# Linear attention over 256 tokens: scores about the middle of each 128 tokens and one block between the halves, in place of chunk states and transposed keys

## The chip, the cores and the metric

The kernel runs on one core of a Trainium2 chip. A core has an engine for matrix products (TensorE, PE in the profile, whose loads of stationary weights are listed apart as PEld), VectorE (DVE), ScalarE (ACT), GpSimd (POOL) and SyncE (SP), which here issues nearly all transfers. Each engine works through its own queue in order, and waits on semaphores for the others. The metric is the device time of one execution in microseconds (us); smaller is better.

## The reference, cut to what matters

One decoder layer over 256 tokens of width 1024: a norm with modulation, a wide projection, two mixing branches, a mixture of 64 experts, and a last norm. The change lies in the first branch, gated linear attention with 4 heads (keys of 128, values of 256):

```python
log_a = jax.nn.log_sigmoid(g_dn @ gate_w2 + gate_b) / GATE_TAU      # per token and key channel
b = jnp.cumsum(gc, axis=3)                  # gc: log_a in chunks of 64 tokens
q_t = qc * jnp.exp(b)
k_t = kc * jnp.exp(-b)
k_s = kc * jnp.exp(b_last - b)
attn = jnp.where(causal, jnp.einsum('nbhid,nbhjd->nbhij', q_t, k_t), 0.0)
o_intra = jnp.einsum('nbhij,nbhjv->nbhiv', attn, vc)
# over the chunks, one after the other, from S = 0:
o_i = jnp.einsum('bhid,bhdv->bhiv', q_i, state)
state = d_i[..., None] * state + jnp.einsum('bhid,bhiv->bhdv', k_i, v_i)
# output: o_intra + o_inter
```

So token t sees token s at or before t through the product of all decays between them. The code scales q by 1/sqrt(128) as well. What follows (norm per head, gate, output products, experts) is the same in both kernels.

## The kernel before, in words

All weights are read from HBM once, in an order fixed by hand. SP's queue holds every load in that order, and a load is issued when its slot in SBUF comes free. The projections run over a list of 88 items, each a 128x1024 block of weights. Each item from 16 on is 24 matmuls of 256 columns (`mm_blk`, L356). Five items ahead of its use (`LA`), a block is split into a high and a low part: `split_h` is a cast on ACT (L340), `split_l` a subtraction on DVE (L347) that also frees the block's ring slot. DVE further does one reduction over a block of the modulation weights in many items (`mod_blk`, L257).

Work between items is hung on item numbers. In the loop over items, `first(b, f)` runs ahead of the splits that stand in item b, `pre(b, f)` after the cast and ahead of the DVE half of the splits, and `at(b, f)` after both and ahead of item b's own matmuls:

```python
run((b, "first"))
for nxt in nxts: split_h(nxt)
if pend: evac(b, *pend)
run((b, "pre"))
for nxt in nxts: split_l(nxt)
run(b)
mm_blk(b, ps[:, i % 2], rhs)
```

The attention is hung on items 16 to 39. `gate0` to `gate4` make `bb`, the running sum of the gate in chunks of 64. `gate5` to `gate8` make three arrays of exponentials on ACT: `eb` (L453) for q, `enb` (L463) for the keys of the scores, and `ekb` (L464, after a subtraction on DVE, L456) for the keys of the states; `decay` holds a chunk's last value. `k_evac` (L720, L721) and `q_evac` (L715) multiply the projections in PSUM by them. Then TensorE transposes the state keys (`gla_kst`, L481), makes the scores of each 128 tokens (`gla_attn`, L494), which DVE copies under a mask (`gla_attn2`, L498), makes three state products (`gla_state`, L506), which ACT and DVE chain up (L513, L515), and the outputs per head: values by scores (L525) and states by queries, one 64-token chunk at a time (L529).

Four PSUM tiles M0 to M3 are handed out in turn by `mt`: the transposes take two, the scores two, the state products of the first two chunks all four, so those wait until the scores have been copied.

After the items follow the router and the experts, in groups of four: a product of 12 loads of 2 MB (`l1_unit`, `l2_unit`, L1044), whose slots are refilled as soon as a product is done with them.

Of the kernel before, what the change touches and what calls it, by code (L numbers as in the profile page):

```python
# [7 lines left out]
F32 = mybir.dt.float32  # L8
# [4 lines left out]
AF = mybir.ActivationFunctionType  # L13
OP = mybir.AluOpType
# [5 lines left out]
TT = 2  # L20
H = 4
# [96 lines left out]
def trunk_kernel(ctx: ExitStack, tc: tile.TileContext, xT: bass.AP, c: bass.AP, modw: bass.AP,  # L118
# [29 lines left out]
    def fl(t):  # L148
        return t.rearrange("p a b -> p (a b)")
# [78 lines left out]
    ident = sm.tile([128, 128], F32, name="ident")  # L228
    V.tensor_scalar(ident, jp, 0.0, None, op0=OP.is_equal)
    cmask = sm.tile([128, 128], I32, name="cmask")  # L230
    V.tensor_scalar(cmask, jp, 0.0, None, op0=OP.is_ge)
    V.memset(cmask[0:64, 64:128], 0)
    tri = sm.tile([128, 128], BF, name="tri")
    V.tensor_scalar(tri, jp, 0.0, None, op0=OP.is_gt)
    trif = sm.tile([128, 128], BF, name="trif")
# [58 lines left out]
    for i in range(2):  # L294
        ps = mt()
# [107 lines left out]
    L = {}  # L403


    t9 = big.tile([128, 4, 1024], F32, name="t9", tag="T9")
    gb = big.tile([128, 4, H, TOK], F32, name="gb", tag="T10")
    la, bb, eb, enb = (t9[:, i].rearrange("p (h t) -> p h t", h=H) for i in range(4))
    L["sr"], L["osq"] = (t9[:, 2 * i:2 * i + 2].rearrange("p a (k t) -> p (a k) t", t=TOK) for i in range(2))
    L["v"] = t8[:, 0].rearrange("p (t d) -> p t d", t=2)  # L410
    L["o"] = gb[:, 2:4].rearrange("p a h t -> p (a h) t")
    ekb, qt, kt_, ks = (gb[:, i] for i in range(4))
    decay = sm.tile([128, H, 4], F32, name="decay")
    b4 = bb.rearrange("p h (c t) -> p (h c) t", t=64)

    def gate0():
        ps = zt(512)
# [32 lines left out]
        V.tensor_tensor_scan(fl(bb), smask, fl(la), 0.0, op0=OP.mult, op1=OP.add)  # L450

    def gate5():
        S.activation(eb, bb, AF.Exp, scale=-1.0 / 16)  # L453

    def gate6():
        V.tensor_sub(ekb.rearrange("p h (c t) -> p (h c) t", t=64),  # L456
                     b4[:, :, 63:64].to_broadcast([128, 16, 64]), b4)

    def gate7():
        V.tensor_copy(decay, eb.rearrange("p h (c t) -> p h c t", t=64)[:, :, :, 63])  # L460

    def gate8():
        S.activation(enb, bb, AF.Exp, scale=1.0 / 16)  # L463
        S.activation(ekb, ekb, AF.Exp, scale=-1.0 / 16)  # L464

    def gla_setup():
        g2 = big.tile([128, 4, 1024], F32, name="gc", tag="T11")
        L["kst"] = g2[:, 0].rearrange("p (t d) -> p t d", t=2)  # L470
        L["at"] = g2[:, 1].rearrange("p (t h i) -> p t h i", t=2, h=H)
        for ch, i in ((1, 2), (2, 3), (3, 0)):
            L["S", ch] = g2[:, i].rearrange("p (h d) -> p h d", h=H)
        G.memset(g2[:, 1], 0.0)

    def gla_kst():
        L["pk"] = []
        for tt in range(TT):
            ps = mt(H, 128)
            for h in range(H):  # L480
                T.transpose(ps[:, h], ks[:, h, 128 * tt:128 * tt + 128], ident)  # L481
            L["pk"].append(ps)

    def gla_kst2():
        for tt in range(TT):
            S.copy(L["kst"][:, tt], fl(L["pk"][tt]))

    def gla_attn():
        L["pa"] = []
        for tt in range(TT):  # L490
# [6 lines left out]
    def gla_attn2(tt):
        V.copy_predicated(L["at"][:, tt], cmask[:, None, :].to_broadcast([128, H, 128]), L["pa"][tt])  # L498

    def gla_state(*chs):  # L500
        for ch in chs:
            L["ps", ch] = [mt(2, 256) for _ in range(2)]
        for h in range(H):
            for ch in chs:
                tt, r = ch // 2, slice(64 * (ch % 2), 64 * (ch % 2) + 64)
                T.matmul(L["ps", ch][h // 2][:, h % 2], L["kst"][r, tt, 128 * h:128 * h + 128],  # L506
                         L["v"][r, tt, 256 * h:256 * h + 256], start=True, stop=True)

    def gla_state2(ch):
        new = L["S", ch + 1]  # L510
        for h in range(H):
            if ch == 0:
                S.copy(new[:, h], L["ps", ch][h // 2][:, h % 2])  # L513
            else:
                V.scalar_tensor_tensor(new[:, h], L["S", ch][:, h], decay[:, h, ch:ch + 1],  # L515
                                       L["ps", ch][h // 2][:, h % 2], op0=OP.mult, op1=OP.add)
# [188 lines left out]
    pk, pq = ([pm.tile([128, 2, TOK], F32, name="m", tag=f"M{2 * j + i}") for i in range(2)] for j in range(2))  # L705
    ps = None
# [5 lines left out]

    def q_evac():
        for j in range(2):
            V.scalar_tensor_tensor(qt[:, 2 * j:2 * j + 2], pq[j], 128.0 ** -0.5, eb[:, 2 * j:2 * j + 2],  # L715
                                   op0=OP.mult, op1=OP.mult)

    def k_evac(j):
        s = slice(2 * j, 2 * j + 2)
        V.tensor_mul(ks[:, s], pk[j], ekb[:, s])  # L720
        V.tensor_mul(kt_[:, s], pk[j], enb[:, s])  # L721

    def b_evac(q, ps):
        if q == 0:
# [142 lines left out]
    o = [0]  # L867
# [82 lines left out]
    pa = ctx.enter_context(tc.tile_pool(name="pa", bufs=2, space=bass.MemoryType.PSUM))  # L950
# [199 lines left out]
    for g in range(NGRP):  # L1150
# [28 lines left out]
        ps = pa.tile([128, D], F32, name="a")  # L1179
# [137 lines left out]
```

## Time and profile before

| | before |
|---|---|
| median of 3 runs | 1206.52 us (1205.83 to 1207.27) |
| profiled execution, its own time | 1206.66 us |
| span of its trace | 1204.8 us |
| PE busy | 902.7 us (75%) |
| DVE busy | 380.0 us (32%) |
| ACT busy | 224.6 us (19%) |
| read from HBM | 475.79 MB, 396 GB/s over the span |
| mean granted TensorE clock | 0.897 of full speed |

The span runs from the first to the last instruction; the execution's own time is 1.86 us longer. "Busy" sums an engine's work over the whole span, so it mixes the projections (to about 297 us) with the experts. In the rows below a time stands in us from the start of the span, and L with a number is a line of the kernel before. One f32 matmul of the code leaves two MATMUL records in the trace, so a group of 8 matmuls reads x16 there.

### The profile page before, as it was taken

How to read it: one execution, taken by the hardware profiler on the slowest of the kernel's cores; microseconds unless marked ns; L12 is line 12 of the kernel's file. 1: busy time of each engine (PE TensorE's matmuls, PEld its weight loads, DVE VectorE, ACT ScalarE, POOL GpSimd, SP SyncE). 2: the span in 40 equal slices, each digit the busy share in tenths (PEclk: the TensorE clock that was granted, in tenths of full speed). 3: DMA queues.
4: the chain of work that ended last, by engine and by line, in shares of the span. 5: the costliest groups of instructions: out<-in, count | busy, mean ns of one | idle time of the engine just before them, and what ended most of it. 6: DMA issues, size and time to landing. Idle time of an engine off the chain costs nothing.

```text
span 1204.8 us, 14633 instructions
## 1 busy us (share of the span) xinstructions
PE 902.7 (75%) x6202; PEld 479.9 (40%) x6202; DVE 380.0 (32%) x718; ACT 224.6 (19%) x375; POOL 3.9 (0%) x15
## 2 busy tenths in 40 slices
PE   9999999999898666666666757576757566757565
PEld 6999999999342212121212212121212111412112
DVE  8968699654431111111111112020202001202103
ACT  6774545433310101010101000000000000100002
POOL 0000000000000000000000000000000000000000
PEclk9999999999999888888888788888888888988888
DMA  9987589978999999999999999999999999999995
GB/s 369 396 333 252 178 301 341 377 272 349 417 428 431 430 431 429 432 431 430 430 430 431 430 431 429 431 430 430 431 429 432 430 432 431 429 430 430 432 427 228
DMA packets 51482, 477.84 MB, mean 397 GB/s; under 512 B 5970, under 2 KB 6098, under 8 KB 27092
## 3 DMA queue, kind: packets, MB, share of 16 engines
q1 hardware_dynamic: 50544, 475.81, 95.4%
q8 instruction: 50, 0.82, 0.2%
q10 hardware_dynamic: 868, 1.05, 0.2%
q14 instruction: 20, 0.16, 0.0%
HBM read 475.79 MB, written 1.05 MB: 396 GB/s over the span
## 4 chain that ended last, share of the span: by engine, by line
DMA 67%; PE 29%; DVE 3%; ACT 0%; issue 0%; DVEq 0%; SPq 0%; ACTq 0%
DMA unit<-in_ew_dram 47%; DMA ring<-in_ew_dram 19%; PE z L356 17%; PE a L1044 3%; PE m L364 2%; PE z L373 2%; PE m L1016 1%; PE m L1071 1%; PE a L1196 0%; PE z L220 0%; PE m L529 0%; PE m L506 0%; PE m L525 0%; PE m L296 0%; DVE xt L257 0%
## 5 line engine op out<-in xcount | busy, mean ns | idle before, releaser
L1044 PE MATMUL a<-unit,xt 128*32 128x512 f32 x1440 | 210.8, 717 | 95.2 <-DMA unit<-in_ew_dram 95.2
L1044 PE MATMUL a<-unit,gt 128*32 128x512 f32 x736 | 119.7, 786 | 70.0 <-DMA unit<-in_ew_dram 69.3
L1044 PEld LDWEIGHTS a<-unit,xt 128*32 128x32 f32 x1440 | 45.0, 122 | 244.0 <-DMA unit<-in_ew_dram 131.5
L356 PE MATMUL z<-hhl,sp 128*128 128x256 f32 x1152 | 140.9, 284 | 0.0
L356 PEld LDWEIGHTS z<-hhl,sp 128*128 128x128 f32 x1152 | 138.9, 192 | 1.6 <-issue 1.5
L1020 ACT ACTIVATE xt<-m,modc,A 128x128 f32<-128x128 f32 x64 | 25.9, 453 | 527.7 <-PE m L1016 526.7
L347 DVE TENSOR_TENSOR sp<-ring,sp 128x1024 fp32r<-128x1024 f32 x88 | 106.9, 1221 | 42.8 <-ACT sp L340 41.8
L1044 PE MATMUL a<-ring,xt 128*32 128x512 f32 x608 | 84.2, 677 | 40.0 <-DMA ring<-in_ew_dram 40.0
L340 ACT CAST sp<-ring 128x1024 fp32r<-128x1024 f32 x88 | 91.4, 1048 | 95.3 <-PE z L356 68.4
L1075 DVE TENSOR_TENSOR wk<-wk,m 128x512 f32<-128x512 f32 (+2 forms) x64 | 41.7, 654 | 196.1 <-PE m L1071 196.1
L1062 DVE TENSOR_TENSOR xt<-a,xt 128x1024 f32<-128x1024 f32 (+3 forms) x19 | 20.0, 1055 | 259.9 <-PE a L1044 253.1
L1044 PEld LDWEIGHTS a<-unit,gt 128*32 128x32 f32 x736 | 24.3, 128 | 154.7 <-DMA unit<-in_ew_dram 99.4
L1016 PEld LDWEIGHTS m<-scr,wk 128*128 128x128 f32 x512 | 60.3, 196 | 21.0 <-issue 20.6
L1016 PE MATMUL m<-scr,wk 128*128 128x128 f32 x512 | 64.0, 283 | 5.6 <-DVE scr L1005 4.9
L1071 PE MATMUL m<-xt,pwt 128*128 128x512 f32 (+2 forms) x136 | 62.7, 603 | 5.3 <-DVE xt L1062 5.3
L1052 DVE TENSOR_TENSOR gt<-gt,a 128x512 f32<-128x512 f32 x16 | 11.0, 688 | 166.3 <-ACT gt L1051 166.3
L257 DVE SCALAR_TENSOR_TENSOR xt<-ring,xt 128x1024 f32<-128x1024 f32 x48 | 58.5, 1219 | 0.3
L1044 PEld LDWEIGHTS a<-ring,xt 128*32 128x32 f32 x608 | 18.6, 117 | 99.2 <-DMA ring<-in_ew_dram 49.8
L1022 DVE TENSOR_SCALAR xt<-m,A,modc 128x128 f32<-128x128 f32 x64 | 23.3, 406 | 105.1 <-PE m L1016 105.1
L1044 PE MATMUL a<-ring,gt 128*32 128x512 f32 x208 | 34.3, 790 | 24.5 <-DMA ring<-in_ew_dram 23.8
L1071 PEld LDWEIGHTS m<-xt,pwt 128*128 128x128 f32 x136 | 25.3, 201 | 49.1 <-issue 36.9
L1051 ACT ACTIVATE gt<-a 128x512 f32<-128x512 f32 x16 | 9.6, 597 | 176.0 <-PE a L1044 176.0
(253 smaller groups left out, 634.9 us busy)
## 6 DMA issues: line engine op xcount, KB each, us to landing
unit<-in_ew_dram SPq DMA_DIRECT2D x136, 2048.0 KB, 38.8
ring<-in_ew_dram SPq DMA_DIRECT2D x48, 2048.0 KB, 38.9
ring<-in_win_dram SPq DMA_DIRECT2D x88, 512.0 KB, 8.0
ring<-in_modw_dram SPq DMA_DIRECT2D x48, 512.0 KB, 6.6
ring<-in_ew_dram SPq DMA_DIRECT2D x12, 512.0 KB, 7.8
unit<-in_el_dram SPq DMA_DIRECT2D x4, 1024.0 KB, 31.5
ring<-in_el_dram SPq DMA_DIRECT2D x4, 512.0 KB, 20.2
unit<-in_el_dram SPq DMA_DIRECT2D x4, 512.0 KB, 11.2
```

Source lines behind the costliest of these rows:

```text
L257: V.scalar_tensor_tensor(scr, st.block("m", i, b), 1.0, cB, op0=OP.mult, op1=OP.mult, accum_out=modc[:, 4 * i + b:4 * i + b + 1])
L340: S.copy(sp(b)[:, 0], st.block("w", n, i))
L347: V.tensor_sub(t[:, 1], st.block("w", n, i), t[:, 0].bitcast(F32))
L356: T.matmul(ps, t[:, ws, k], rhs[rs][:, k], start=(clear and k == 0 and n == 0), stop=(k == KT - 1 and n == 2), skip_group_check=True)
L364: T.matmul(pb[:, h % 2], t[:, ws, h], hl[rs][:, kk], start=(kk == 0 and h % 2 == 0 and n == 0), stop=(kk == KT - 1 and h % 2 == 1 and n == ...
L373: T.matmul(pv[tt][hh], hl[rs][:, kk, 128 * tt:128 * tt + 128], t[:, ws, 512 * hh:512 * hh + 512], start=(kk == 0 and n == 0), stop=(kk == ...
L1016: T.matmul(ps[j], acc[:, tt, f:f + 128], Pm[:, tt], start=(tt == 0), stop=(tt == 1))
L1020: S.activation(xg[:, k], ps[j], AF.Identity, bias=B2[:, k:k + 1], scale=A2[:, k:k + 1])
L1022: V.tensor_scalar(xg[:, k], ps[j], A2[:, k:k + 1], B2[:, k:k + 1], op0=OP.mult, op1=OP.add)
L1044: T.matmul(ps[32 * j:32 * j + 32, 512 * hh:512 * hh + 512], lhsT[:, 32 * j:32 * j + 32], w[:, j, 512 * hh:512 * hh + 512], start=first, st ...
L1071: T.matmul(ps[:, :w], pwt[:, tt], X["y"][:, s], start=True, stop=True)
L1075: V.tensor_add(total[:, tt, s], total[:, tt, s], ps[:, :w])
```

## The change

The chunks of 64 with their running sums stay up to `bb`. From there:

- In each 128 tokens q and k are scaled about the middle (the end of its first 64) instead of the start of their own chunk: `wE` is the distance to the middle in the first half, `bb` itself in the second, and `eq` and `ek` are the exponentials of it with either sign. So one scaled q (`qx`) and one scaled k (`kx`) serve all scores within 128 tokens, also those between its two chunks.
- The block of scores between the first 128 tokens (keys) and the second (queries) comes from `kd` and `qd`: `kx` of the first half times the decay from its middle to its end, and `qx` of the second times the decay of its first chunk (`gla_far`).
- `gla_attn` makes the scores of each 128 tokens in two matmuls per head (keys 0 to 63 by queries 0 to 63, all keys by queries 64 to 127), then the block between the halves in one per head. DVE copies the first kind under the causal mask (`gla_near`, two copies per 128 tokens), ACT copies the block whole (`gla_cross`).
- Each output is then values by scores alone: the values of the first 128 tokens by 256 query columns, those of the second by 128 (`gla_o`).
- The transposes, the copies of transposed keys, the state products, their chaining on ACT and DVE, one array of exponentials, and the second product per key evacuation go.

```diff
-    V.memset(cmask[0:64, 64:128], 0)
...
     def gate5():
-        S.activation(eb, bb, AF.Exp, scale=-1.0 / 16)
+
+        V.tensor_sub(wE, half(bb, 0)[:, :, 63:64].to_broadcast([128, 8, 64]), half(bb, 0))
 
     def gate6():
-        V.tensor_sub(ekb.rearrange("p h (c t) -> p (h c) t", t=64),
-                     b4[:, :, 63:64].to_broadcast([128, 16, 64]), b4)
-
-    def gate7():
-        V.tensor_copy(decay, eb.rearrange("p h (c t) -> p h c t", t=64)[:, :, :, 63])
-
-    def gate8():
-        S.activation(enb, bb, AF.Exp, scale=1.0 / 16)
-        S.activation(ekb, ekb, AF.Exp, scale=-1.0 / 16)
+        for d, sg in ((ek, -1.0), (eq, 1.0)):
+            S.activation(half(d, 0), wE, AF.Exp, scale=sg / 16)
+            S.activation(half(d, 1), half(bb, 1), AF.Exp, scale=-sg / 16)
+        for c in range(2):
+            S.activation(decay[:, c], bb[:, :, 64 * c + 127], AF.Exp, scale=-1.0 / 16)
...
+    def gla_far():
+        for d, x, c, o in ((kd, kx, 0, 0), (qd, qx, 1, 128)):
+            V.tensor_mul(d, x[:, :, o:o + 128], decay[:, c, :, None].to_broadcast([128, H, 128]))
+
+    def gla_attn():
+        L["pa"] = []
+        a, b = slice(0, 128), slice(128, 256)
+        for k, q in ((kx[:, :, a], qx[:, :, a]), (kx[:, :, b], qx[:, :, b]), (kd, qd)):
             ps = mt(H, 128)
             for h in range(H):
-                T.transpose(ps[:, h], ks[:, h, 128 * tt:128 * tt + 128], ident)
...
+                if k is kd:
+                    T.matmul(ps[:, h], k[:, h], q[:, h], start=True, stop=True)
+                    continue
+                T.matmul(ps[0:64, h, 0:64], k[:, h, 0:64], q[:, h, 0:64], start=True, stop=True, skip_group_check=True)
+                T.matmul(ps[:, h, 64:128], k[:, h], q[:, h, 64:128], start=True, stop=True, skip_group_check=True)
             L["pa"].append(ps)
...
+    def gla_near(tt):
+        t, ps = (L["at0"][:, :, 0:128], L["at1"])[tt], L["pa"][tt]
+        for n, c in ((64, 0), (128, 64)):
+            V.copy_predicated(t[:n, :, c:c + 64], cmask[:n, None, c:c + 64].to_broadcast([n, H, 64]), ps[:n, :, c:c + 64])
+
+    def gla_cross():
+        S.copy(L["at0"][:, :, 128:256], L["pa"][2])
...
         for a in range(2):
             f = 256 * h + 128 * a
-            for tt in range(TT):
-                s = slice(128 * tt, 128 * tt + 128)
-                T.matmul(ps[:, a, s], vt[:, tt, f:f + 128], L["at"][:, tt, h],
-                         start=(a == 0 and tt == 0), stop=False, skip_group_check=True)
-            for ch in range(1, 4):
-                s = slice(64 * ch, 64 * ch + 64)
-                T.matmul(ps[:, a, s], L["S", ch][:, h, 128 * a:128 * a + 128], qt[:, h, s],
-                         start=False, stop=(a == 1 and ch == 3), skip_group_check=True)
+            T.matmul(ps[:, a], vt[:, 0, f:f + 128], L["at0"][:, h], start=(a == 0), stop=False, skip_group_check=True)
+            T.matmul(ps[:, a, 128:256], vt[:, 1, f:f + 128], L["at1"][:, h], start=False, stop=(a == 1),
+                     skip_group_check=True)
...
-    at(21, gate6)
-    first(22, gate5)
-    first(23, gate8)
-    at(23, gate7)
+    at(21, gate5)
+    first(22, gate6)
     at(23, lambda: k_evac(0))
     at(24, lambda: k_evac(1))
     at(25, lambda: q_evac())
     at(25, gla_setup)
+    at(26, gla_far)
     at(40, st.free, "T12")
-    at(27, gla_kst)
-    at(28, gla_attn)
-    first(28, gla_kst2)
-    pre(29, gla_attn2, 0)
-    pre(29, gla_attn2, 1)
-    at(29, gla_state, 0, 1)
-    first(30, gla_state2, 0)
-    pre(30, gla_state2, 1)
-    at(31, gla_state, 2)
-    pre(32, gla_state2, 2)
+    at(27, gla_attn)
+    first(28, gla_cross)
+    pre(29, gla_near, 0)
+    pre(29, gla_near, 1)
     at(33, gla_o, 0)
     at(33, gla_o, 1)
...
     def k_evac(j):
         s = slice(2 * j, 2 * j + 2)
-        V.tensor_mul(ks[:, s], pk[j], ekb[:, s])
-        V.tensor_mul(kt_[:, s], pk[j], enb[:, s])
+        V.tensor_mul(kx[:, s], pk[j], ek[:, s])
```

On ACT, in items 21 to 23 (t_181, t_180: the tile of `bb` and the exponentials; t_126, t_125: the projections' results; gb: the tile of the scaled q and k). Before:

```order
L453 ACT_TABLE_LOAD [waits DVE_49]
L453 ACTIVATE t_181<-t_181 128x1024 [waits Activation_49]
L340 CAST sp<-ring 128x1024 [waits DMAHW7_49,PE_49]
L711 COPY t_126<-z 128x512 [waits PE_49]
L463 ACTIVATE t_181<-t_181 128x1024
L464 ACTIVATE gb<-gb 128x1024 [waits DVE_49]
L340 CAST sp<-ring 128x1024 [waits DMAHW1_49,PE_49]
```

and now:

```order
L463 ACT_TABLE_LOAD
L463 ACTIVATE t_180<-gb 128x8x64 [waits DVE_49]
L464 ACTIVATE t_180<-t_180 128x8x64 [waits Activation_49]
L463 ACTIVATE t_180<-gb 128x8x64
L464 ACTIVATE t_180<-t_180 128x8x64
L466 ACTIVATE decay<-t_180 128x4 x2
L339 CAST sp<-ring 128x1024 [waits DMAHW7_49,PE_49]
L683 COPY t_125<-z 128x512 [waits PE_49]
L339 CAST sp<-ring 128x1024 [waits DMAHW1_49,PE_49]
```

All exponentials now stand ahead of the cast of item 27, where one stood there and two behind it; the first waits for DVE's subtraction, and the table load no longer waits for DVE.

On DVE, in items 21 to 26 (L347 and L346: the splits of items 27 on; m: the projections of q and k in PSUM). Before:

```order
L456 TENSOR_TENSOR gb<-t_181 128x1024 [waits DVE_49]
L347 TENSOR_TENSOR sp<-ring,sp 128x1024 [waits DMAHW7_49,PE_49,Activation_49]
L257 SCALAR_TENSOR_TENSOR xt,modc<-ring,xt 128x1024 [waits DMAHW0_49]
L347 TENSOR_TENSOR sp<-ring,sp 128x1024 [waits DMAHW1_49,PE_49,Activation_49]
L460 COPY decay<-t_181 128x16
L720 TENSOR_TENSOR gb<-m,gb 128x512 [waits DVE_49]
L721 TENSOR_TENSOR gb<-m,t_181 128x512
L347 TENSOR_TENSOR sp<-ring,sp 128x1024 [waits DMAHW2_49,PE_49,Activation_49]
L720 TENSOR_TENSOR gb<-m,gb 128x512
L721 TENSOR_TENSOR gb<-m,t_181 128x512
L347 TENSOR_TENSOR sp<-ring,sp 128x1024 [waits DMAHW3_49,PE_49,Activation_49]
L715 SCALAR_TENSOR_TENSOR gb<-m,t_181 128x512 x2
```

and now:

```order
L459 TENSOR_TENSOR gb<-t_180 128x512 [waits DVE_49]
L346 TENSOR_TENSOR sp<-ring,sp 128x1024 [waits DMAHW7_49,PE_49,Activation_49]
L256 SCALAR_TENSOR_TENSOR xt,modc<-ring,xt 128x1024 [waits DMAHW0_49]
L346 TENSOR_TENSOR sp<-ring,sp 128x1024 [waits DMAHW1_49,PE_49,Activation_49]
L692 TENSOR_TENSOR gb<-m,t_180 128x512
L346 TENSOR_TENSOR sp<-ring,sp 128x1024 [waits DMAHW2_49,PE_49,Activation_49]
L692 TENSOR_TENSOR gb<-m,t_180 128x512
L346 TENSOR_TENSOR sp<-ring,sp 128x1024 [waits DMAHW3_49,PE_49,Activation_49]
L687 SCALAR_TENSOR_TENSOR gb<-m,t_180 128x512 x2
L346 TENSOR_TENSOR sp<-ring,sp 128x1024 [waits DMAHW4_49,PE_49,Activation_49]
L479 TENSOR_TENSOR gb<-gb,decay 128x512 [waits DVE_49] x2
```

The subtraction is half as long, each key evacuation is one product instead of two, and the two products of `gla_far` (L479) follow one split behind the queries.

On TensorE, in items 27 to 33, 24 matmuls of L356 (L355 now) to an item (hhl: the normed input, gc: scores, states and transposed keys, t_126 and t_125: values). Before:

```order
L356 MATMUL z<-hhl,sp 128x256 x240
L481 MATMUL m<-ident,gb 128x128 x8
L356 MATMUL z<-hhl,sp 128x256 x24
L494 MATMUL m<-gb 128x128 x8
L356 MATMUL z<-hhl,sp 128x256 x24
L506 MATMUL m<-t_126,gc 128x256 x8
L356 MATMUL z<-hhl,sp 128x256 x48
L506 MATMUL m<-t_126,gc 128x256 x4
L356 MATMUL z<-hhl,sp 128x256 x48
L525 MATMUL m<-gc,t_126 128x128 x2
L529 MATMUL m<-gb,gc 128x64 x3
```

and now (the pair L490, L491 stands there eight times, the pair L507, L508 four times on each side of item 33):

```order
L355 MATMUL z<-hhl,sp 128x256 x240
L490 MATMUL m<-gb 64x64
L491 MATMUL m<-gb 128x64
...
L488 MATMUL m<-gb 128x128 x4
L355 MATMUL z<-hhl,sp 128x256 x144
L507 MATMUL m<-gc,t_125 128x256
L508 MATMUL m<-gc,t_125 128x128
```

All scores now stand ahead of item 27, where the transposes stood, one item earlier than before; nothing stands between items 27 and 32; and a pair of outputs is two matmuls in place of five.

## Rows read from the trace of the kernel before

**Rows 1.** The page's chain of work that ended last, shares by engine.

```profile
DMA 67%; PE 29%; DVE 3%; ACT 0%; issue 0%; DVEq 0%; SPq 0%; ACTq 0%
```

**Rows 2.** That chain in order of time: start, us, what.

```profile
66.30 28.24 PE z L356 x236
...
104.42 0.74 DVE gc L498
105.20 1.99 PE m L506 x14
...
113.12 1.92 PE m L506 x8
...
121.44 0.62 PE m L529 x6
122.05 0.50 PE m L525 x4
...
365.42 29.28 DMA unit<-in_ew_dram
```

**Rows 3.** Windows: us, busy PE, PEld, DVE, ACT, POOL; PEclk, DMA share, GB/s.

```profile
100.00:105.00 5.00, 4.11 (x32) 3.57 (x30) 4.96 (x8) 1.33 (x2) 0.00 (x0) 1.00 0.89 275
...
110.00:120.00 10.00, 10.00 (x77) 9.36 (x76) 6.06 (x9) 4.14 (x5) 0.00 (x0) 1.00 0.65 206
...
365.00:400.00 35.00, 28.56 (x222) 10.69 (x215) 6.60 (x13) 2.35 (x6) 0.00 (x0) 0.97 1.01 430
```

**Rows 4.** Timeline of TensorE, 94 to 104 us: start, us, engine, line.

```profile
94.92 1.04 PE L481 MATMUL m<-ident,gb 128*128 128x128 f32 x8
95.72 3.11 PE L356 MATMUL z<-hhl,sp 128*128 128x256 f32 x24
98.67 1.95 PE L494 MATMUL m<-gb 128*128 128x128 f32 x16
100.37 3.11 PE L356 MATMUL z<-hhl,sp 128*128 128x256 f32 x24
103.41 0.70 PE L506 MATMUL m<-t,gc 64*128 64x256 f32 x2
```

**Rows 5.** Timeline of DVE, 83 to 98 us.

```profile
83.48 1.20 DVE L347 TENSOR_TENSOR sp<-ring,sp 128x1024 fp32r<-128x1024 f32 x1
84.60 1.22 DVE L456 TENSOR_TENSOR gb<-t 128x1024 f32<-128x1024 f32 x1
...
88.11 1.22 DVE L257 SCALAR_TENSOR_TENSOR xt<-ring,xt 128x1024 f32<-128x1024 f32 x1
...
96.18 1.28 DVE L715 SCALAR_TENSOR_TENSOR gb<-m,t 128x512 f32<-128x512 f32 x2
```

**Rows 6.** Timeline of ACT, 83 to 87 us.

```profile
83.65 1.28 ACT L453 ACT_TABLE_LOAD   x1 [3.43 <-DVE t L450]
84.94 1.06 ACT L453 ACTIVATE t<-t 128x1024 f32<-128x1024 f32 x1
85.91 1.03 ACT L340 CAST sp<-ring 128x1024 fp32r<-128x1024 f32 x1
```

**Rows 7.** Groups of ACT by line and form: busy us, mean ns.

```profile
L567 ACT CAST ohl<-gb 128x512 fp32r<-128x512 f32 x4 | 2.5, 615 | 0.0
...
L669 ACT ACTIVATE dum<-epsc 128x1 f32<-128x1 f32 x1 | 0.2, 203 | 0.0
```

**Rows 8.** Windows of 1 us in the first group of experts; columns as in rows 3.

```profile
322.00:323.00 1.00, 0.56 (x8) 0.00 (x0) 0.00 (x0) 0.37 (x1) 0.00 (x0) 1.00 1.11 475
323.00:324.00 1.00, 0.00 (x0) 0.00 (x0) 0.74 (x2) 0.23 (x1) 0.00 (x0) 1.00 0.99 426
...
326.00:327.00 1.00, 1.00 (x8) 0.22 (x4) 0.93 (x10) 0.00 (x0) 0.00 (x0) 0.57 0.99 426
327.00:328.00 1.00, 1.00 (x9) 0.22 (x5) 0.93 (x5) 0.00 (x0) 0.00 (x0) 0.50 0.92 393
...
329.00:330.00 1.00, 1.00 (x12) 0.20 (x8) 0.97 (x2) 0.00 (x0) 0.00 (x0) 0.73 1.07 459
```

More of the change, by code (lines that the diff above doesn't have):

```diff
@@ L407, in trunk_kernel @@
     gb = big.tile([128, 4, H, TOK], F32, name="gb", tag="T10")
-    la, bb, eb, enb = (t9[:, i].rearrange("p (h t) -> p h t", h=H) for i in range(4))
+    la, bb, eq, ek = (t9[:, i].rearrange("p (h t) -> p h t", h=H) for i in range(4))
     L["sr"], L["osq"] = (t9[:, 2 * i:2 * i + 2].rearrange("p a (k t) -> p (a k) t", t=TOK) for i in range(2))
@@ L411, in trunk_kernel, with half @@
     L["o"] = gb[:, 2:4].rearrange("p a h t -> p (a h) t")
-    ekb, qt, kt_, ks = (gb[:, i] for i in range(4))
-    decay = sm.tile([128, H, 4], F32, name="decay")
-    b4 = bb.rearrange("p h (c t) -> p (h c) t", t=64)
+    wE, qx, kx = gb[:, 0, 0:2].rearrange("p h t -> p (h t)"), gb[:, 1], gb[:, 3]
+    wE = wE.rearrange("p (a t) -> p a t", t=64)
+    kd, qd = (gb[:, 2].rearrange("p h t -> p (h t)")[:, 512 * i:512 * i + 512].rearrange("p (h t) -> p h t", h=H)
+              for i in range(2))
+    decay = sm.tile([128, 2, H], F32, name="decay")
+    def half(t, c):
+        return t.rearrange("p h (a c t) -> p (h a) c t", c=2, t=64)[:, :, c]
     def gate0():
@@ L468, in gla_setup @@
+        for c in range(2):
+            S.activation(decay[:, c], bb[:, :, 64 * c + 127], AF.Exp, scale=-1.0 / 16)
     def gla_setup():
         g2 = big.tile([128, 4, 1024], F32, name="gc", tag="T11")
[L470 to L477, printed above, removed]
-        for tt in range(TT):
+        L["at0"] = g2[:, 0].rearrange("p (h i) -> p h i", h=H)
@@ new lines, in gla_setup @@
+        L["at1"] = g2[:, 1, 0:512].rearrange("p (h i) -> p h i", h=H)
+        G.memset(L["at0"][:, :, 0:128], 0.0)
+        G.memset(L["at1"], 0.0)
+    def gla_far():
[5 more added lines that the diff above has]
+        for k, q in ((kx[:, :, a], qx[:, :, a]), (kx[:, :, b], qx[:, :, b]), (kd, qd)):
@@ L479, in gla_kst @@
             ps = mt(H, 128)
             for h in range(H):
-                T.transpose(ps[:, h], ks[:, h, 128 * tt:128 * tt + 128], ident)
[L482 to L490, printed above, removed]
-            s = slice(128 * tt, 128 * tt + 128)
-            ps = mt(H, 128)
-            for h in range(H):
-                T.matmul(ps[:, h], kt_[:, h, s], qt[:, h, s], start=True, stop=True)
-            L["pa"].append(ps)
@@ L497, in gla_attn2 @@
[L497 to L516, printed above, removed]
+                if k is kd:
+                    T.matmul(ps[:, h], k[:, h], q[:, h], start=True, stop=True)
+                    continue
@@ L522, in gla_o @@
             f = 256 * h + 128 * a
-            for tt in range(TT):
-                s = slice(128 * tt, 128 * tt + 128)
-                T.matmul(ps[:, a, s], vt[:, tt, f:f + 128], L["at"][:, tt, h],
-                         start=(a == 0 and tt == 0), stop=False, skip_group_check=True)
-            for ch in range(1, 4):
-                s = slice(64 * ch, 64 * ch + 64)
-                T.matmul(ps[:, a, s], L["S", ch][:, h, 128 * a:128 * a + 128], qt[:, h, s],
-                         start=False, stop=(a == 1 and ch == 3), skip_group_check=True)
+            T.matmul(ps[:, a], vt[:, 0, f:f + 128], L["at0"][:, h], start=(a == 0), stop=False, skip_group_check=True)
+            T.matmul(ps[:, a, 128:256], vt[:, 1, f:f + 128], L["at1"][:, h], start=False, stop=(a == 1),
+                     skip_group_check=True)
         L["po", h] = ps
@@ L714, in q_evac @@
         for j in range(2):
-            V.scalar_tensor_tensor(qt[:, 2 * j:2 * j + 2], pq[j], 128.0 ** -0.5, eb[:, 2 * j:2 * j + 2],
+            V.scalar_tensor_tensor(qx[:, 2 * j:2 * j + 2], pq[j], 128.0 ** -0.5, eq[:, 2 * j:2 * j + 2],
                                    op0=OP.mult, op1=OP.mult)
```

## The prediction

> **What bounds the kernel now.** I read the chain of waits first, then windows of the stretch that the change touches, then the timelines of three engines there. By the chain 67% of the span is DMA and 29% TensorE [rows 1]. In order of time the two do not alternate: up to 362 us the chain runs almost wholly through TensorE, and from 365.42 us on the transfers of expert weights end it [rows 2]. The windows say the same: at 365 to 400 us the DMA engines move 430 GB/s and are full, while at 110 to 120 us they move 206 GB/s, although TensorE is busy for all of that stretch [rows 3]. There the loads wait for slots, and slots come free at TensorE's pace.
>
> So a microsecond taken from TensorE before the loads fill the DMA engines makes every later load start that much earlier, and the end should move by the same amount. A shorter DVE or ACT instruction gives nothing by itself; it counts where TensorE waits for it. That happens once in the attention: the state products begin at 103.41 us, stop, and go on at 105.20 us, because DVE's masked copy of the scores (L498) starts at 104.42 us only, and the products need the PSUM tiles that it frees [rows 2, 4].
>
> **What is removed.** Transposes: 94.92 to 95.72, 0.80 us. Old scores: 98.67 to 100.37, 1.70 us, or 0.106 us for each of 16 records of 128 columns [rows 4]. State products: from 103.41 to 105.20 + 1.99 = 107.19, which is 3.78 us with the stop in it, and 1.92 us for the third chunk [rows 2, 4]. Outputs: a pair is 0.50 + 0.62 us, and there are 8 (4 heads, two halves of the values): 8.96 us [rows 2]. Together 0.80 + 1.70 + 3.78 + 1.92 + 8.96 = 17.16 us of TensorE's line.
>
> The chaining of states on ACT and DVE, the second key products and the copies of transposed keys go too. Outside the stop they lie beside TensorE, so I cost them at nothing. They matter only through the times at which the new scores can start.
>
> **What is added: the outputs.** A pair is now one matmul of 256 columns and one of 128, two records each. For 128 columns I take 0.106 to 0.125 us a record (the 1.70/16 above; 0.50/4 of L525). For 256 columns the lower bound is twice 0.106, the upper 0.24, which is 1.92/8 of the third state product [rows 2]. A pair is 0.64 to 0.73 us, eight are 5.1 to 5.8; I take 5.4, between, since these weights have 128 rows and those of L506 64.
>
> **What is added: the scores.** They stand where the transposes stood, at 94.92 us, and need `kx` and `qx`. When are these ready? I follow the order of rows on ACT and DVE with the durations of before.
>
> DVE's subtraction starts as before at 84.60 us; half as long, it ends near 85.3 (one of two operations of 512 columns is 1.28/2 us at L715) [rows 5]. The exponentials wait for it. The table load does not wait any more: before, it ran at 83.65 only when DVE was through, and took 1.28 us [rows 6]; now it has room ahead of 85.3. An ACT instruction of 512 columns takes 0.615 us [rows 7], and successive ones overlap by about 0.1 us (84.94 + 1.06 against 85.91 [rows 6]). Four of them, the second waiting for the first, end at about 87.6, and two of four columns, at most 0.2 us each by the small one in [rows 7], bring ACT to 87.9. There the cast of item 27 starts, which began at 85.91 before: 2.0 us later. Its 1.03 us over [rows 6], DVE goes on at 88.95.
>
> DVE then does a split (1.12 us from start to start, 83.48 to 84.60), a reduction (1.2), a split, half of the keys (0.6), a split, the other half, a split, and the queries in two parts of 0.6 [rows 5]. That is 88.95 + 1.12 + 1.2 + 1.12 + 0.6 + 1.12 + 0.6 + 1.12 = 95.8, the first half of q at 96.5, the second at 97.1. Before, the queries started at 96.18 [rows 5]: what DVE saves on the keys and what it waits longer for the cast nearly cancel. The first two heads need the first half alone. So TensorE, there at 94.92, stands until about 96.6: a new wait of 1.7 us. Queued behind it are the splits' consumers, item 27 and all that follows; the casts on ACT that wait for TensorE to leave a slot start later too, but five items of lead cover that (an item is 24 x 28.24/236 = 2.87 us [rows 2]).
>
> The 8 pairs of near scores are 32 records of 64 columns. L529 has that form: 0.62/6 = 0.103 us a record [rows 2], no less than 128 columns take, so its weight loads set the pace. Half of the new ones load 64 columns of weights only. If that halves their time, 32 cost 2.5 us, if not, 3.3; I take 2.9, to 99.5 us.
>
> [...]
>
> Meanwhile DVE does a split and the two products of `gla_far`: 97.1 + 1.12 + 0.6 + 0.7 = 99.5. So the block between the halves just meets its operands, and its 8 records of 0.106 us bring the scores to 100.4 us. A faster near part would gain nothing, since DVE then ends last. Scores: 100.4 − 94.92 = 5.5 us.
>
> The copies of the scores no longer hold anyone: the outputs stand six items on, some 17 us later. Two memsets on POOL replace one, in item 25, four items ahead of the copies. SP's loads keep their order.
>
> **Sum.** 17.16 − 5.4 − 5.5 = 6.2 us less. The profiled execution took 1206.66 us by its own time, 0.14 us above the median of the runs. Forecast: 1206.66 − 6.2 = 1200.5 us.
>
> **The rivals.**
>
> *The clock falls in the new wait.* [...] Against it: the stop at 104 us, hardly shorter than the new one, left the clock at 1.00 [rows 3]. [...]
>
> *A longer wait for q.* If ACT's exponentials over columns in pieces of 64 cost more, or the table load still follows the subtraction (1.28 us), the wait is 3 us: 4.9 us saved, 1201.8; with dear outputs and near scores (0.4 us each), 1202.6.
>
> *No wait at all.* Without the later cast, the first half of q would be ready at 96.18 + 0.6 − 1.2 (two key products) − 0.6 (half a subtraction) = 95.0 us [rows 5], `gla_far` at 95.6 + 1.12 + 1.3 = 98.0 and the scores at 98.9. Then 7.7 us are saved, 8.0 with cheap outputs: 1198.7. [rows 6] speak against it: the cast stands behind all exponentials.
>
> *The gain is not handed on.* If the loads bound the end by their own rate from earlier than I think, the change ends at 1206.5, give or take. For it: 67% of the chain is DMA [rows 1]. Against it: 206 GB/s at 110 to 120 us against 430 at the end [rows 3].
>
> [...]
>
> **How the numbers follow.** Forecast case 0.58; the clock 0.15; a longer wait 0.10; no wait 0.07; not handed on 0.07; slower 0.03. Faster by over 0.2% are the first four, 0.90; the same 0.07; slower 0.03. The range takes in the clock, the longer wait with dear matmuls and a part of their sum, and on the other side most of the case without a wait: 1198.8 to 1203.6 us.
>
> **What would show it.** Right: TensorE idle once for 1 to 2.5 us just ahead of the near scores, released by the q product on DVE; none ahead of the outputs; a pair of outputs near 0.67 us; item 34 starting at 100.4 + 7 x 2.87 + 5.4 = 125.9 us; from there the same work at the same distances, the switch of the chain to DMA at 365.4 − 6.2 = 359 us. Wrong: a granted clock under 1.00 between 95 and 130 us, a second stop ahead of the block between the halves, or later stretches that give the 6 us back as lower DMA rates. What would break the forecast most is a wait ahead of the near scores much longer than DVE's queue explains.

## The result, and the profile after

| | before | changed |
|---|---|---|
| median of 6 runs | 1207.17 us | 1213.14 us (1209.57 to 1213.60) |
| ratio to before, 95% interval | | 1.0051 [1.0041, 1.0061] |
| span of the profiled execution | 1204.8 us | 1211.7 us |
| mean granted TensorE clock | 0.897 | 0.886 |
| read from HBM | 475.79 MB, 396 GB/s | 475.79 MB, 394 GB/s |

The change makes the kernel 6 us slower where 6 us faster was forecast. Lines in the rows below are those of the kernel that they come from. In the changed one L355 is the matmuls of the items, L490 and L491 the near scores (64 and 128 columns of weights), L488 the far block, L507 and L508 the outputs, L1015 the experts.

The chain of waits of the changed kernel in order of time (start, us, what) answers to [rows 2]:

```profile
66.68 25.80 PE z L355 x215
...
96.04 0.61 DVE gb L687
96.69 0.33 PE m L490 x2
...
104.02 1.81 PE m L488 x8
105.84 18.45 PE z L355 x144
...
132.40 5.75 PE z L355 x48
...
363.84 31.91 DMA unit<-in_ew_dram
```

In the same view of the kernel before, item 34 starts here:

```profile
132.74 5.80 PE z L356 x48
```

The reader sees the new wait (L490 follows DVE's L687), scores that take until 105.84 us, and item 34 at 132.40 us. Before, item 34 starts at 132.74 us, though its items began 0.38 us earlier (66.30 [rows 2] against 66.68). So the whole attention, 17 us of removed work and all, gave some 0.7 us in these two executions. And the 7 us by which the span is longer arise later still: the chain leaves TensorE at 363.84 us, earlier than before, but that load lands at 395.75 us against 365.42 + 29.28 = 394.70 [rows 2], and from there on the loads alone make the chain, up to 1180.5 us (in the kernel before up to 1172.8).

The windows (columns as in [rows 3]) show both places:

```profile
95.00:100.00 5.00, 3.77 (x21) 2.88 (x21) 5.00 (x7) 1.61 (x3) 0.00 (x0) 0.82 0.97 333
100.00:105.00 5.00, 5.00 (x22) 4.18 (x23) 3.00 (x5) 0.00 (x0) 0.00 (x0) 0.50 0.81 243
105.00:110.00 5.00, 5.00 (x31) 5.00 (x31) 0.00 (x0) 0.78 (x2) 0.00 (x0) 0.66 0.48 185
...
365.00:400.00 35.00, 27.29 (x205) 9.24 (x194) 6.13 (x12) 1.99 (x4) 0.00 (x0) 0.95 1.01 426
```

From about 98 to 108 us TensorE is granted 0.50 of full speed: (1 − 0.82) x 5 / 0.5 + 5 + (1 − 0.66) x 5 / 0.5 = 10.2 us at the low level, so 5.1 us of work at the full clock is lost. And at 365 to 400 us the DMA engines, as full as before, move 426 GB/s instead of 430 [rows 3].

On TensorE's timeline the near scores begin at one pace and go on at another:

```profile
96.69 0.33 PE L490 MATMUL m<-gb 128*64 128x64 f32 x2 [1.23 <-DVE gb L687]
96.95 0.43 PE L491 MATMUL m<-gb 128*128 128x64 f32 x2
97.32 0.33 PE L490 MATMUL m<-gb 128*64 128x64 f32 x2
...
98.82 0.48 PE L490 MATMUL m<-gb 128*64 128x64 f32 x2
...
99.85 0.48 PE L490 MATMUL m<-gb 128*64 128x64 f32 x2
...
124.13 0.60 PE L507 MATMUL m<-gc,t 128*128 128x256 f32 x2
124.56 0.38 PE L508 MATMUL m<-gc,t 128*128 128x128 f32 x2
124.78 0.60 PE L507 MATMUL m<-gc,t 128*128 128x256 f32 x2
```

A pair of L490 and L491 takes 97.32 − 96.69 = 0.63 us at full clock, where I had 4 x 0.09 = 0.36; at the low clock it takes 99.85 − 98.82 = 1.03. The pair of outputs behind (0.43 + 0.22 by start times) is as forecast.

### The profile page after: what moved, and what is told of

Read it like the earlier page. It is cut to its first block, busy times and chain, and to the rows that moved or that the text cites. A ratio compares the mean times of both kernels' runs of the same rounds, so it can differ in the third digit from the quotient of the medians.

```text
span 1211.7 us, 14506 instructions
## 1 busy us (share of the span) xinstructions
PE 909.3 (75%) x6146; PEld 480.2 (40%) x6146; DVE 375.8 (31%) x710; ACT 222.2 (18%) x373; POOL 4.0 (0%) x16
## 3 DMA queue, kind: packets, MB, share of 16 engines
HBM read 475.79 MB, written 1.05 MB: 394 GB/s over the span
## 4 chain that ended last, share of the span: by engine, by line
DMA 67%; PE 29%; DVE 2%; ACT 0%; issue 0%; DVEq 0%; SPq 0%; ACTq 0%
DMA unit<-in_ew_dram 48%; DMA ring<-in_ew_dram 20%; PE z L355 17%; PE a L1015 3%; PE m L363 2%; PE z L372 2%; PE m L987 1%; PE m L1042 1%; PE a L1167 0%; PE z L220 0%; PE m L491 0%; PE m L295 0%; PE m L311 0%; PE m L507 0%; ACT wk L1181 0%
## 5 line engine op out<-in xcount | busy, mean ns | idle before, releaser
L1015 PE MATMUL a<-unit,xt 128*32 128x512 f32 x1440 | 211.8, 718 | 106.7 <-DMA unit<-in_ew_dram 106.7
L1015 PE MATMUL a<-unit,gt 128*32 128x512 f32 x736 | 123.9, 812 | 62.1 <-DMA unit<-in_ew_dram 57.7
L1015 PEld LDWEIGHTS a<-unit,xt 128*32 128x32 f32 x1440 | 44.9, 122 | 252.5 <-DMA unit<-in_ew_dram 140.0
L355 PE MATMUL z<-hhl,sp 128*128 128x256 f32 x1152 | 141.4, 285 | 0.0
L355 PEld LDWEIGHTS z<-hhl,sp 128*128 128x128 f32 x1152 | 140.1, 194 | 0.9 <-issue 0.8
L346 DVE TENSOR_TENSOR sp<-ring,sp 128x1024 fp32r<-128x1024 f32 x88 | 106.8, 1220 | 47.7 <-ACT sp L339 47.7
L1015 PE MATMUL a<-ring,xt 128*32 128x512 f32 x608 | 83.5, 671 | 34.3 <-DMA ring<-in_ew_dram 34.3
L339 ACT CAST sp<-ring 128x1024 fp32r<-128x1024 f32 x88 | 91.6, 1048 | 95.8 <-PE z L355 61.8
L1015 PEld LDWEIGHTS a<-unit,gt 128*32 128x32 f32 x736 | 24.2, 131 | 149.1 <-DMA unit<-in_ew_dram 90.7
L1015 PEld LDWEIGHTS a<-ring,xt 128*32 128x32 f32 x608 | 18.1, 116 | 95.9 <-DMA ring<-in_ew_dram 48.7
L1015 PE MATMUL a<-ring,gt 128*32 128x512 f32 x208 | 34.0, 784 | 24.6 <-DMA ring<-in_ew_dram 24.6
```

The source lines that it names most:

```text
L339: S.copy(sp(b)[:, 0], st.block("w", n, i))
L346: V.tensor_sub(t[:, 1], st.block("w", n, i), t[:, 0].bitcast(F32))
L355: T.matmul(ps, t[:, ws, k], rhs[rs][:, k], start=(clear and k == 0 and n == 0), stop=(k == KT - 1 and n == 2), skip_group_check=True)
L1015: T.matmul(ps[32 * j:32 * j + 32, 512 * hh:512 * hh + 512], lhsT[:, 32 * j:32 * j + 32], w[:, j, 512 * hh:512 * hh + 512], start=first, st ...
```

## Experiments

What moved the loads' rate was not in the diff's lines on the attention, but in one on `decay`: that tile went from 64 to 32 bytes per partition. All small tiles lie ahead of the large ones, so in the built program the ring of weight blocks begins at byte 15840 of each partition instead of 15872 (31 x 512), and all large tiles behind it, those of the expert weights with them (16384 bytes each), start 32 bytes short of a multiple of 512, where they started at one. Theory A says that this is the slower loading. Rival B says that the rate belongs to the chip or to the new timing. For the attention, C says that the wait for q made the clock fall, D and later E that the score matmuls did.

**The 32 bytes given back**

```diff
     decay = sm.tile([128, 2, H], F32, name="decay")
+    sm.tile([128, 8], F32, name="pad")
```

> The changed kernel with one unused tile of 32 bytes per partition behind decay, so that the ring and all tiles of expert weights lie where they lay in the kernel before. Theory A (the loads write more slowly because the smaller decay moved every weight tile by 32 bytes): from 400 to 1100 us the DMA engines move 430 GB/s again instead of 427, and the time falls by about 6 us, to 1205.5 to 1207.5 us. Theory B (the rate is a matter of the chip or of the loads' timing after the attention): 427 GB/s and 1210 to 1213.5 us as in the changed kernel. By both the clock still falls ahead of the scores, and the attention ends about where it did.

1204.98 us (11 runs), 0.9984 [0.9975, 0.9993] of before, a little under the range of A. The windows of its profile:

```profile
95.00:100.00 5.00, 3.77 (x24) 3.00 (x24) 5.00 (x7) 2.21 (x3) 0.00 (x0) 0.88 0.89 297
100.00:105.00 5.00, 5.00 (x21) 4.06 (x22) 3.59 (x6) 0.00 (x0) 0.00 (x0) 0.50 0.86 300
...
400.00:1100.00 700.00, 460.13 (x2823) 144.14 (x2825) 100.67 (x227) 37.23 (x82) 0.00 (x0) 0.84 1.01 430
```

The instructions are those of the changed kernel in the same order, only addresses differ; the clock falls in the same place, and 8.2 us are back, with 430 GB/s in the long stretch, where the changed kernel has this:

```profile
400.00:1100.00 700.00, 458.68 (x2801) 142.38 (x2800) 97.00 (x219) 37.20 (x82) 0.00 (x0) 0.84 1.01 427
```

**The kernel before, shifted to the same remainder**

```diff
     decay = sm.tile([128, H, 4], F32, name="decay")
+    sm.tile([128, 120], F32, name="pad")
```

> The kernel before with one unused tile of 480 bytes per partition behind decay, so that its weight tiles start at the remainder by 512 bytes that those of the changed kernel have. Nothing else is changed. Theory A: 427 GB/s from 400 to 1100 us and about 7 us more than before, 1213 to 1215 us. Theory B: 430 GB/s and no change, 1206 to 1208 us.

1214.85 us, 1.0067 [1.0054, 1.0081]; the same window:

```profile
400.00:1100.00 700.00, 456.13 (x2803) 141.45 (x2806) 97.28 (x219) 38.00 (x84) 0.00 (x0) 0.84 1.01 427
```

So A holds and B falls: the addresses alone cost 8.1 us (1214.85 − 1206.79), with no change in the attention at all. The rates account for nearly all of it: unrounded, the bytes that landed from 400 to 1100 us give 430.5 GB/s in the kernel before and 426.8 here, and 0.9% of the some 890 us from 305 us on is 7.7 us. A packet of 16384 bytes took 612 ns on the mean before and 617 ns here.

**Which boundary counts**: the kernel before with 256 bytes more and with 64 bytes more

```diff
     decay = sm.tile([128, H, 4], F32, name="decay")
+    sm.tile([128, 64], F32, name="pad")
```

```diff
     decay = sm.tile([128, H, 4], F32, name="decay")
+    sm.tile([128, 16], F32, name="pad")
```

> The kernel before with an unused tile of 256 bytes per partition behind decay: every weight tile starts 256 bytes past a multiple of 512. If what counts is a start at a multiple of 256 bytes: 430 GB/s and no change, 1206 to 1208 us. If it is a multiple of 512: 427 GB/s and 1213 to 1215.5 us.

> The kernel before with an unused tile of 64 bytes per partition behind decay: every weight tile starts 64 bytes past a multiple of 512. If a start at a multiple of 64 bytes is enough: 430 GB/s, 1206 to 1208 us. If a multiple of 256 or 512 is needed: 427 GB/s, 1213 to 1215.5 us.

256 bytes: 1207.13 us, 1.0002 [0.9993, 1.0011]. 64 bytes: 1213.14 us, 1.0050 [1.0036, 1.0064]. Their windows, the 256 bytes first:

```profile
400.00:1100.00 700.00, 461.07 (x2824) 143.10 (x2826) 100.84 (x227) 37.18 (x82) 0.00 (x0) 0.84 1.01 431
```

```profile
400.00:1100.00 700.00, 456.01 (x2808) 141.94 (x2807) 97.85 (x220) 37.55 (x84) 0.00 (x0) 0.85 1.01 428
```

With the large tiles 256 bytes past a multiple of 512 the loads move 431 GB/s and the time stays; at 64 past it they move 428, and the time is 6.3 us longer (1213.14 − 1206.85). What these runs move is the place in SBUF that the loads write. Starts at remainders of 480 and 64 are slow here and those at 0 and 256 are not; a boundary of 256 bytes fits that, and one of 128 as well, which was not tried.

**Scores one item later**, with the 32 bytes and without

```diff
-    at(27, gla_attn)
-    first(28, gla_cross)
-    pre(29, gla_near, 0)
-    pre(29, gla_near, 1)
+    at(28, gla_attn)
+    first(29, gla_cross)
+    pre(30, gla_near, 0)
+    pre(30, gla_near, 1)
```

> The changed kernel with the 32 bytes and the scores one item later: attention scores in item 28, the copy of the block in 29, the masked copies in 30. TensorE then has an item to work on while DVE ends q. Theory C (the wait of TensorE for q made the clock fall, and the low clock ate the gain): no wait, granted clock 1.00 from 95 to 130 us, the last outputs end about 6 us earlier than in the changed kernel, and with theory A the time is 1199.5 to 1202 us. Theory D (the short score matmuls themselves lower the clock): the clock falls without the wait, and the time is 1203 to 1207 us.

> The changed kernel with the scores one item later, weight tiles as in the changed kernel. Theories A and C: clock at 1.00, 427 GB/s, 1206 to 1208.5 us, so the two losses add up. B and C: 1206 to 1208 us and the same time as the run with the 32 bytes. D: 1209 to 1213 us.

With the bytes 1199.02 us, 0.9936 [0.9922, 0.9949], a little better than C; without 1208.85 us, 1.0016 [1.0006, 1.0027], a little above what A and C together gave. The wait is gone in both, and yet the clock falls in the profile of the first, behind the near scores. Its windows and its timeline of TensorE:

```profile
95.00:100.00 5.00, 5.00 (x40) 4.39 (x38) 5.00 (x7) 2.60 (x4) 0.00 (x0) 1.00 0.97 360
100.00:105.00 5.00, 5.00 (x30) 4.46 (x31) 4.85 (x9) 0.49 (x1) 0.00 (x0) 0.78 0.76 238
```

```profile
97.70 0.33 PE L491 MATMUL m<-gb 128*64 128x64 f32 x2
...
102.59 1.82 PE L489 MATMUL m<-gb 128*128 128x128 f32 x8
```

In the profile of the second it stays:

```profile
100.00:105.00 5.00, 5.00 (x38) 4.39 (x39) 5.00 (x8) 0.59 (x1) 0.00 (x0) 1.00 0.80 272
```

So C, though its times are met, is not the whole cause: here the clock fell without a wait (0.78 at 100 to 105 us). Nor is one profile the rule: the execution profiled of the first is its slowest of five (1201.22 us), that of the second the second fastest of its nine (1206.80 us). What the first also shows is the price of the near scores without a wait and at full clock: 102.59 − 97.70 = 4.9 us, or 0.153 us a record, where 0.103 was the most that I had allowed.

**Near scores in one matmul per head**, late and at the change's place, both with the 32 bytes (the masked quarter is computed too)

```diff
-                if k is kd:
-                    T.matmul(ps[:, h], k[:, h], q[:, h], start=True, stop=True)
-                    continue
-                T.matmul(ps[0:64, h, 0:64], k[:, h, 0:64], q[:, h, 0:64], start=True, stop=True, skip_group_check=True)
-                T.matmul(ps[:, h, 64:128], k[:, h], q[:, h, 64:128], start=True, stop=True, skip_group_check=True)
+                T.matmul(ps[:, h], k[:, h], q[:, h], start=True, stop=True)
```

> As the run with the 32 bytes and the scores one item later, and the near scores of each 128 tokens made by one matmul of 128 columns per head in place of two of 64 (the quarter that the mask drops is computed too and not copied). Theory E (the two narrow forms are dear by themselves, 0.15 us a record at full clock, and keep TensorE's activity so low that the clock falls in some runs): the near scores take 1.7 to 1.8 us instead of 4.9, the clock stays at 1.00, and the time is 1194.5 to 1196.5 us. Rival F (the narrow form costs little in the end, since DVE's products for the far block bind the scores, and the clock falls by chance): 1198 to 1199.5 us.

> The changed kernel with the 32 bytes and with one matmul of 128 columns per head for the near scores; they stay ahead of item 27, so TensorE still waits for q. Theory C1 (the wait alone makes the clock fall): granted clock under 1.00 between 97 and 105 us, 1199.5 to 1202 us. Theory E (the narrow matmuls do it, the wait of 1.2 us does not suffice): clock at 1.00 all through, two short waits of TensorE (for q, and for the far block's operands), 1196 to 1198.5 us.

Late: 1195.38 us, 0.9904 [0.9889, 0.9919]. All scores take 100.42 − 97.83 = 2.6 us, and the clock stays:

```profile
97.83 2.84 PE L488 MATMUL m<-gb 128*128 128x128 f32 x24
100.42 14.64 PE L355 MATMUL z<-hhl,sp 128*128 128x256 f32 x120
...
122.93 5.28 PE L355 MATMUL z<-hhl,sp 128*128 128x256 f32 x42
```

```profile
100.00:105.00 5.00, 5.00 (x44) 5.00 (x44) 4.96 (x9) 1.63 (x2) 0.00 (x0) 1.00 0.85 255
```

At the change's place: 1199.13 us, 0.9934 [0.9920, 0.9947], above the 1196 to 1198.5 of E and just below C1's range, but not by C1's mechanism, as its timeline and windows show:

```profile
97.17 2.20 PE L488 MATMUL m<-gb 128*128 128x128 f32 x16 [1.24 <-DVE gb L684]
100.10 1.16 PE L488 MATMUL m<-gb 128*128 128x128 f32 x8 [0.73 <-DVE gb L480]
101.02 17.52 PE L355 MATMUL z<-hhl,sp 128*128 128x256 f32 x144
```

```profile
95.00:100.00 5.00, 3.13 (x24) 2.66 (x23) 5.00 (x8) 2.09 (x3) 0.00 (x0) 1.00 0.87 301
100.00:105.00 5.00, 4.90 (x41) 4.90 (x42) 3.48 (x6) 1.54 (x2) 0.00 (x0) 1.00 0.82 271
```

There TensorE waits twice, for q and for the far block's operands. By the timeline that costs 2.5 us against the late run: 1.24 us ahead of the scores, and scores of 101.02 − 97.17 = 3.85 us instead of 2.6. The medians lie 3.75 us apart; the intervals of the two allow both. TensorE is idle for longer than in the changed kernel (5.00 − 3.13 = 1.87 us at 95 to 100 us against 5.00 − 3.77 = 1.23), and the clock stays at 1.00.

**The form of the near scores**, one execution each: sorted by width, and with one width of weights

```diff
                 T.matmul(ps[0:64, h, 0:64], k[:, h, 0:64], q[:, h, 0:64], start=True, stop=True, skip_group_check=True)
+            for h in range(H if k is not kd else 0):
                 T.matmul(ps[:, h, 64:128], k[:, h], q[:, h, 64:128], start=True, stop=True, skip_group_check=True)
```

```diff
-                T.matmul(ps[0:64, h, 0:64], k[:, h, 0:64], q[:, h, 0:64], start=True, stop=True, skip_group_check=True)
+                T.matmul(ps[:, h, 0:64], k[:, h], q[:, h, 0:64], start=True, stop=True, skip_group_check=True)
```

> As the run with the 32 bytes and the scores one item later, with the near scores of each 128 tokens sorted: first the four heads with 64 columns of weights, then the four with 128. Theory G (each change between a load of 64 columns and one of 128 keeps the loads from running ahead of the matmuls): near scores 16 x 0.053 to 0.103 + 16 x 0.103 = 2.5 to 3.3 us instead of 4.9. Rival H (these forms are as dear in any order): 4.5 to 4.9 us.

> As the run with the 32 bytes and the scores one item later, where the narrow matmul too loads all 128 columns of weights and fills all 128 partitions (queries 0 to 63 only): 32 records of 64 columns of one form, as in the state outputs of before. Theory G: 32 x 0.103 = 3.3 us. Rival H (64 columns against 128 of weights is dear here in any form): 4.5 us or more.

1198.19 and 1197.56 us (the kernel before beside them: 1206.08). TensorE, sorted first:

```profile
97.82 0.68 PE L491 MATMUL m<-gb 128*64 128x64 f32 x8
98.43 1.11 PE L493 MATMUL m<-gb 128*128 128x64 f32 x8
99.46 0.68 PE L491 MATMUL m<-gb 128*64 128x64 f32 x8
100.07 1.10 PE L493 MATMUL m<-gb 128*128 128x64 f32 x8
101.01 1.11 PE L489 MATMUL m<-gb 128*128 128x128 f32 x8
```

```profile
98.17 0.33 PE L491 MATMUL m<-gb 128*128 128x64 f32 x2
...
101.69 1.11 PE L489 MATMUL m<-gb 128*128 128x128 f32 x8
```

3.2 and 3.5 us against 4.9. The sorted run has the very matmuls of the late one (16, or 32 records) in another order, so it is the alternation that is dear here: H falls, and G's times hold, with the second run a little above its 3.3. That the alternation acts through the loads is G's guess; these times do not show it. The clock stays at 1.00 in both; in the sorted run:

```profile
100.00:105.00 5.00, 5.00 (x45) 4.93 (x44) 4.96 (x9) 0.67 (x2) 0.00 (x0) 1.00 0.79 234
```

**The clock once more**: the wait alone and the alternating form alone, the kernels of two runs above unchanged

> A second look at the run with whole near scores ahead of item 27, for the clock alone. Theory E (the wait does not lower it): 1.00 in all windows from 95 to 110 us. Theory C1: below 1.00 in some.

> A second look at the run with the 32 bytes and the scores one item later (narrow forms, no wait), for the clock alone. Theory E: below 1.00 in some looks at this kernel; so far in one, and not in the one look at its twin without the 32 bytes.

1200.65 and 1201.42 us, one execution each. Windows, the wait alone first:

```profile
95.00:100.00 5.00, 3.12 (x24) 2.64 (x22) 5.00 (x8) 2.07 (x3) 0.00 (x0) 1.00 0.85 286
```

```profile
100.00:105.00 5.00, 5.00 (x25) 4.14 (x26) 5.00 (x8) 0.00 (x0) 0.00 (x0) 0.62 0.82 262
105.00:110.00 5.00, 5.00 (x32) 5.00 (x32) 0.20 (x3) 0.82 (x2) 0.00 (x0) 0.69 0.96 324
```

Over all profiles of the new attention: alternating widths behind a wait, low in 2 of 2; alternating widths without a wait, 2 of 3; the wait with whole scores, 0 of 2; neither, 0 of 3. With the wait the low stretch also came earlier (98 us in the changed kernel, 101 and 103 us without the wait) and lasted 10.2 us in both profiles instead of 3.4 and 6.9, so in these the wait adds to it. These are few executions, and how often the clock falls in each kernel is not known.

## Why the prediction was wrong

**What it left out.** The sum had no term for where tiles lie. "From there the same work at the same distances" was the step that failed: from 305 us on the work was the same, but the large tiles lay 32 bytes short of a multiple of 512, the loads into them ran at 427 GB/s instead of 430, and that costs 8.1 to 8.2 us, shown both ways. This is larger than the forecast gain and turned the sign. No rival held it; "not handed on" ended at no change. The diff showed the cause in the one line on `decay`, which I read as a detail. Of the signs that the prediction had set out for being wrong two came: a clock under 1.00 between 95 and 130 us, and lower DMA rates later.

**Where the gain itself went.** Without the 8 us the forecast would have failed too: with the 32 bytes given back the kernel is only 1206.79 − 1204.98 = 1.8 us faster than before, where 6.2 were forecast. Item 34 was to start at 125.9 us and starts at 132.40, later by about all that was to be gained: 4.4 us in the near scores, 1.0 in the far block at the low clock (1.81 against 0.85), 1.2 in the items behind it (18.45 against 6 x 2.87). And of the 1.8 us some 0.8 come from no term of the prediction. The last lines of the two chains, before and changed:

```profile
1199.32 0.40 DVE wk L1247
```

```profile
1206.95 0.40 DVE wk L1218
```

From the end of this instruction to the end of the span pass 1204.8 − 1199.72 = 5.1 us before and 1211.7 − 1207.35 = 4.35 us in the changed kernel; it is 5.1 to 5.2 us in all four profiles with the attention of before and 4.2 to 4.4 us in all ten with the new one. Why the end is shorter is open.

**The bound.** That TensorE sets the pace to about 360 us and that time taken from it moves the end holds: in the late run with whole scores item 34 starts at 122.93 us, 9.6 earlier than the 132.55 of before, and the median falls by 11.5 us. On the timeline of before:

```profile
132.55 5.99 PE L356 MATMUL z<-hhl,sp 128*128 128x256 f32 x48
```

Of the 1.9 us between the two, some 0.8 are the shorter end; the rest is not traced.

**What is removed.** 17.16 us was right within the trace's own rounding: 17.16 less 2.6 for that run's scores and 5.2 for its outputs is 9.4, against 9.6 measured.

**Outputs.** 5.4 us forecast, 8 x 0.65 = 5.2 measured.

**The times of q.** ACT and DVE went as worked out, as their timelines in the changed kernel show:

```profile
80.61 1.28 ACT L463 ACT_TABLE_LOAD   x1
85.71 0.63 ACT L463 ACTIVATE t<-gb 128x512 f32<-128x512 f32 x1 [3.81 <-DVE gb L459]
...
88.00 1.03 ACT L339 CAST sp<-ring 128x1024 fp32r<-128x1024 f32 x1
```

```profile
95.96 1.28 DVE L687 SCALAR_TENSOR_TENSOR gb<-m,t 128x512 f32<-128x512 f32 x2
...
98.29 1.28 DVE L479 TENSOR_TENSOR gb<-gb,decay 128x512 f32<-128x512 f32 x2
```

The table load runs ahead of the subtraction, the cast starts at 88.00 (87.9 forecast), the queries at 95.96 (95.8), and the far products end at 99.57 (99.5). The near scores start at 96.69 (96.6).

**Near scores.** The mis-sized term: 2.9 us forecast, bounded by 3.3; 104.02 − 96.69 = 7.3 measured. Of that 4.9 is the alternation of widths at full clock, and 2.4 the clock. The bound came from L529, where all loads have one width. Even sorted, the run shows 0.076 us a narrow record ((98.43 − 97.82)/8) and 0.118 to 0.129 a wide one ((101.01 − 100.07)/8, (99.46 − 98.43)/8). That 64 columns of weights halve a record's time, on which the lower end of 2.5 us rests, no run shows: 0.076 us is some six tenths of the wide one's.

**The clock.** I gave it 0.15, with the wait as its cause. The range takes in a loss of some 1.7 us, which is what the low stretch of [rows 8] comes to, 3.4 us at 0.50 of full speed in the experts; behind the wait no run shows that size. It came and cost 5.1 us by the granted clock, 4.5 by the starts of matmuls (2.4 in the near scores, 0.9 in the far block, 1.2 in the items). Its cause was not the wait alone: the alternating matmuls sufficed without the wait in 2 of 3 profiles, and the wait without them in none of 2. At half the clock the 6.2 us of the forecast would have been gone after 12.4 us; the low stretch lasted 10.2, so the clock alone would not have made the kernel slower, to which 0.03 was given. TensorE was busy throughout behind the scores (5.00 of 5.00 us at 105 to 110 us); all the same the clock stayed low for some 2.5 us of the items there.

**The sum again, from runs.** From the changed kernel to the best one: addresses 8.2 us, alternating scores with their clock 1204.98 − 1199.13 = 5.9, the waits 1199.13 − 1195.38 = 3.75 (2.5 by the timelines); together the 17.8 us between 1213.14 and 1195.38. As steps from median to median they have to add up to that; what supports them is that the first was found the other way round as well (8.1), and that the timelines show the second as 6.2 us: with the 32 bytes alone the scores last from 97.29 to 106.08 us, 4.9 us longer than the 3.85 of whole scores at the same place, and the six items behind them take 1.3 us longer.

## What to carry to other kernels

Before forecasting a change, look at what it does to the addresses behind it: a small tile that shrinks moves every later tile, and here, where loads bound the end, tiles that start 32 bytes short of a multiple of 512 cost 8 us of 1207, more than the edit was to gain. A count of short matmuls says little: with widths in turn they cost half as much again here as sorted (4.9 us against 3.2), and in 4 of 5 profiles the clock fell with them and was low for the long ones behind them too, so that a product of one shape with a masked quarter was cheaper here than the exact one in two (1195.38 us against 1199.02). Hang a consumer where its operands are ready by the slowest queue, not where its predecessor stood: one item later was worth 3.75 us by the medians, 2.5 by the timelines.

## What the runs showed of the hardware that was not expected

- Loads at 430 GB/s fell to 427 with every large destination tile 480 bytes past a multiple of 512 in SBUF, and to 428 at 64 past it (1.0067 and 1.0050 of the time before); 256 past it cost nothing (1.0002 [0.9993, 1.0011]).
- 32 f32 records of 64 columns took 4.9 us with loads of 64 and 128 columns in turn, 3.2 sorted by width, 3.5 all with 128.
- The granted clock fell while TensorE was busy by the profile for every us (0.78 and 0.62 in the windows at 100 to 105 us of two runs without a wait, and 0.50 from 103 to 106 us of the first), and stayed at 1.00 in 5 us of which 1.9 were idle (whole scores behind the wait). Which property of the alternating matmuls the clock answers to is open; that it is TensorE's activity, as E has it, no run shows.
